# Projections and v products take turns over four PSUM banks until the retention's first step

## The chip, the core and the metric

The kernel runs on one core of one Trainium2 chip. Times are device microseconds of a whole execution. The engines are named as in the profile: PE is TensorE (PEld its weight loads), DVE is VectorE, ACT is ScalarE, POOL is GpSimd, SP issues transfers.

## What is computed

A model of two layers over 512 tokens of width 1024, in float32. Each layer normalises its input, projects it, runs three kinds of attention side by side (a retention with 4 heads in chunks of 128, a sparse attention with 4 heads that keeps the best 128 keys by an indexer's score, and a dilated attention with 8 heads), mixes them through an output matrix, and ends with an MLP.

```python
def hybrid_layer(x, attn_norm_w, w_in, ret_norm_w, kv_norm_w, w_uk, w_uv, w_out, mlp_norm_w, w_up, w_down, pos):
    h = rms_norm(x, attn_norm_w)
    proj = h @ w_in
    ret_cols, dsa_cols, dil_cols = jnp.split(proj, _offsets((RET_COLS, DSA_COLS, DIL_COLS)), axis=-1)
    mixed = jnp.concatenate([retention_mixer(ret_cols, ret_norm_w, pos),
                             dsa_mixer(dsa_cols, kv_norm_w, w_uk, w_uv),
                             dilated_mixer(dil_cols)], axis=-1)
    x = x + mixed @ w_out
    h = rms_norm(x, mlp_norm_w)
    return x + jnp.square(jax.nn.relu(h @ w_up)) @ w_down
```

## The kernel before

Every float32 operand is held as two parts, a rounded one (hi) and its remainder (lo), and each product is three matmuls (hi by hi, hi by lo, lo by hi). A projection (`proj`, L791) is one PSUM tile of 128 columns of weights by 512 tokens: 8 blocks of the inner dimension, 24 matmuls of 512 columns (`wform`, L329). A v product of the dilated heads (`dil_v`, L537) is one tile of 128 tokens by 256 columns: 24 matmuls of 256 columns (`tform`, L339); a call makes four of them, for four blocks of tokens.

PSUM's eight banks are three pools, made at L139 to L141: `mm` with two banks, `at` with four (scores, transposes, products of the heads), `rt` with two. The retention (`ret_tile`, L648) takes all its tiles from `rt`, and so do two of the four v products of each `dil_v`. All projections take `mm`. A bank is free for the next tile when its last reader is done. For a query (`evac_q`, L413) these are two steps of ACT (L423) and two of DVE (L424); for a key (`evac_k`, L428) two of ACT (L436) and two of DVE (L438), with two transfers that ACT issues; for a gate (`gate`, L634) a tanh on ACT (L644) and a step of DVE (L645), then one of POOL (L646); for a v product (`evac_v`, L514) a copy into a work buffer and a rounding, both on ACT (L520, L524), after which POOL takes the remainder from the work buffer (L526). There are three work buffers (pool `p`, `PB` = 3 at L50), which the heads' outputs and the gates use too.

The work of the attention is written head by head (loop in `attention`). Ahead of it stand the token parts, the indexer, the first selection round of the sparse attention (`topk`, L597, DVE only: L602 and L603) and `dil_v` for the first four heads, then query 0 and key 0. After the scores of head h the loop writes the steps that the list `FILL` (L53) names for it: query 1 after head 0; query 2, key 1 and key 2 after head 1; gate 0 after head 2; the second `dil_v` and gate 1 after head 3; key 3 after head 4; query 3 and the retention's own projection after head 5. Then come the products of the head before, as many steps of the retention as `RET` (L54) gives (none before h = 5, four there), and rounds of the selection.

The order on the engines is not that of the text: a planner builds each engine's queue ahead of time from priorities (position in the text plus the offsets of `PR`, L72) and its own estimate of when inputs and buffers are there. Each engine then runs its queue in order, and waits where an input or a buffer isn't ready.

Of the kernel before, what the change touches and what calls it, by code (L numbers as in the profile page):

```python
# [51 lines left out]
C = {  # L52
    'FILL': 'q1,q2 k1 k2,g0,d g1,k3,q3 r,v s0,w,s1,',  # L53
    'RET': (0, 0, 0, 0, 0, 4, 0, 3, 0, 1, 3, 1, 0),  # L54
    'TOPK': (1, 1, 0, 4, 0, 10, 0),
    'POOL_LO': ('dv', 'o', 'sq', 'rg', 'rqk', 'dq', 'dk', 'ukv'),
    'LSPLIT': 2,
    'HOLD': 6,
    'KS': ((4, 6), (0, 2)),
    'SK': 1,  # L60
# [63 lines left out]
class Kern:  # L124
# [412 lines left out]
    def dil_v(self, L, act, g):  # L537
        us = [(self.unit((L, "dv", g, k)), (k, k + 1, k + 2, k + 3)) for k in (0, 4)]
        for t in range(NT):
            ps = self.mm() if t < 2 else self.rt_bank()  # L540
            self.tform(us, act, t, ps, 256)
            self.evac_dil(ps[:, 0:256], g, t)
        self.done(2)
# [238 lines left out]
    def latent_k(self, L, pr):  # L782
# [5 lines left out]
            self.done()  # L788
        return self.evac_k(ps)

    def proj(self, key, act, cols=P):  # L791
        ps = self.mm()
        self.wform(self.unit(key), act, cols, ps, cols)
        self.done()
        return ps
# [34 lines left out]
    def attention(self, L, act):  # L830
        nc = self.nc
        A = self.A
        sc = None
        self.rt = [self.t(self.pmix, [P, 2, 1024], F32, "mix") for _ in range(2)]
        self.vd, self.sg, self.ct, self.vs, self.rqk_done = {}, None, None, None, False
        self.masks = self.t(self.psc, [P, N_CST - N_C1], F32, "masks")
        nc.sync.dma_start(self.masks, A["cst"][:, N_C1:])
# [54 lines left out]
        def out_part(h, t, ks, last=False):  # L892
            ps = self.mm()
            self.tform([(self.unit((L, "o", h, k)), (k, k + 1)) for k in ks], mix, t, ps)
            self.add_x(t, h, ps)
# [4 lines left out]
        for h in range(12 + C["SK"]):  # L900
            if h < 12:
                if h == 8:
                    self.bias(sc)
                with self.prio("hs", h):
                    self.head_s(heads[h // 2], h % 2)
            for f in fill.pop(0) if fill else ():
                with self.prio("fill", f):
                    steps[f]()
            if h == 8 + C["SK"]:
                for t in range(NT):  # L910
                    self.load_x(t, self.xd if L else A["x"])
                mix = [m0, None] + self.md
            if h >= 8 + C["SK"]:
                for _ in range(C["WO"]):
                    if wo and wo[0] not in hold:
                        assert 0 not in C["KS"][0] or m0_done
                        with self.prio("wo", h):
                            out_part(*wo.pop(0), C["KS"][0])
                            if wo and wo[0] == (1, 0):
                                self.done(len(C["KS"][0]))  # L920
            if h >= C["SK"]:
                with self.prio("hv", h):
                    self.head_v(heads[(h - C["SK"]) // 2], (h - C["SK"]) % 2)
            for _ in range(C["RET"][h] if h < 13 else 0):
                with self.prio("ret", h):
                    next(rets, None)
            if h < 6:
                with self.prio("topk", h):
                    self.topk(sc, C["TOPK"][h + 1])
# [200 lines left out]
```

## Time and profile before

| | us |
|---|---|
| median of 3 executions | 1236.36 |
| lowest, highest | 1236.02, 1240.37 |
| the profiled execution | 1236.08 |
| its span, first to last instruction | 1234.1 |
| PE busy (98% of the span) | 1207.2 |
| DVE busy (75%) | 921.4 |
| ACT busy (55%) | 679.2 |
| POOL busy (38%) | 472.4 |

The profile is of one execution. An engine's busy time is the time in which it has an instruction under way; a wait is the idle time just before an instruction, put down to the one that released it. The two layers repeat each other: in layer 0 the part from query 0 to the MLP's first matmul lies between 75 and 309.7 us, in layer 1 between 681 and 917.

### The profile page before, as it was taken

The page shows a single profiled execution, that of the slowest core. Times are in us where ns is not written, and L with a number is a line of the kernel's source. Part 1 is how long each engine was busy: PE and PEld are TensorE (multiplying, and loading weights), DVE is VectorE, ACT ScalarE, POOL GpSimd, SP SyncE. Part 2 cuts the span into 40 slices and gives each one's busy share as a digit, 9 for nine tenths or more (in the row PEclk, how much of TensorE's full clock was granted, in tenths as well). Part 3 has the DMA queues.
Part 4 walks back from the last instruction along what each step waited for, and adds up shares of the span by engine and source line. Part 5 has one row for each costly group of instructions (what it writes and reads, how often), then busy time and mean ns, then how long its engine had stood idle before and what let it go on. Part 6 is the DMA issues. An engine that isn't in the chain of part 4 may idle for free.

```text
span 1234.1 us, 16904 instructions
## 1 busy us (share of the span) xinstructions
PE 1207.2 (98%) x6116; PEld 1027.6 (83%) x6116; DVE 921.4 (75%) x1582; ACT 679.2 (55%) x1241; POOL 472.4 (38%) x461
## 2 busy tenths in 40 slices
PE   7999999999999999999999999999999999999997
PEld 5988888889888888888889888888898888888886
DVE  5599957776875966858866997687769668587596
ACT  6645758745644535535566456686465354354454
POOL 3453748553412304214224546664534032140232
PEclk9999999999999999999999999999999999999999
DMA  7432324215244061260153323231180622514201
GB/s 217 120 83 72 95 69 121 86 53 188 85 137 137 1 215 58 69 184 16 35 166 102 95 71 96 91 120 53 52 256 1 205 68 69 176 30 140 82 1 69
DMA packets 142180, 122.73 MB, mean 99 GB/s; under 512 B 6801, under 2 KB 114065, under 8 KB 142098
## 3 DMA queue, kind: packets, MB, share of 16 engines
q1 hardware_dynamic: 140178, 118.52, 31.9%
q10 hardware_dynamic: 1920, 3.15, 1.0%
q8 instruction: 48, 0.79, 0.3%
q14 instruction: 34, 0.28, 0.1%
HBM read 114.31 MB, written 4.19 MB: 96 GB/s over the span
## 4 chain that ended last, share of the span: by engine, by line
PE 85%; DVE 12%; ACT 1%; issue 1%; DMA 1%; SPq 0%; POOL 0%; POOLq 0%; DVEq 0%; ACTq 0%
PE mm L336 35%; PE mm L348 15%; PE rt L1036 14%; PE at L1036 7%; PE mm L1036 3%; DVE sc L603 3%; DVE top L602 3%; PE at L352 2%; PE at L491 2%; PE at L444 1%; PE at L443 1%; DVE ph L462 1%; PE at L336 1%; DVE Q L424 1%; DMA raw<-in_w_in_dram 1%
## 5 line engine op out<-in xcount | busy, mean ns | idle before, releaser
L336 PE MATMUL mm<-act,w 128*128 128x512 f32 (+2 forms) x2352 | 516.1, 377 | 3.1 <-DVE Q L424 3.1
L336 PEld LDWEIGHTS mm<-act,w 128*128 128x128 f32 x2352 | 424.4, 188 | 79.8 <-issue 3.9
L286 POOL TENSOR_TENSOR w<-raw,w 128x512 fp32r<-128x512 f32 (+1 forms) x124 | 160.0, 1313 | 99.2 <-ACT w L278 74.0
L278 ACT CAST w<-raw 128x1024 fp32r<-128x1024 f32 (+1 forms) x138 | 142.9, 1037 | 79.2 <-PE rt L1036 27.6
L1036 PE MATMUL rt<-w,U 128*128 128x512 f32 x768 | 183.2, 389 | 0.0
L286 DVE TENSOR_TENSOR w<-rd,w 128x1024 fp32r<-128x1024 f32 x112 | 144.7, 1304 | 50.0 <-ACT w L278 50.0
L286 DVE TENSOR_TENSOR w<-raw,w 128x1024 fp32r<-128x1024 f32 (+1 forms) x76 | 94.0, 1238 | 107.5 <-ACT w L278 107.2
L1036 PEld LDWEIGHTS rt<-w,U 128*128 128x128 f32 x768 | 144.1, 188 | 29.9
L993 POOL TENSOR_TENSOR st<-s 128x256 f32<-128x256 f32 x32 | 39.1, 1223 | 330.1 <-ACT s L982 325.3
L278 ACT CAST w<-rd 128x1024 fp32r<-128x1024 f32 x112 | 117.6, 1050 | 83.4 <-PE rt L1036 41.7
L348 PE MATMUL mm<-w,act 128*128 128x456 f32 (+2 forms) x576 | 118.4, 351 | 3.0 <-DVE act L400 1.8
L348 PEld LDWEIGHTS mm<-w,act 128*128 128x128 f32 x576 | 96.4, 189 | 15.2 <-DVE act L400 2.8
L348 PE MATMUL mm<-w,mix 128*128 128x512 f32 x384 | 97.3, 401 | 0.6 <-DVE Q L424 0.5
L1036 PE MATMUL at<-w,U 128*128 128x512 f32 (+1 forms) x396 | 97.7, 386 | 0.0
L304 DVE TENSOR_TENSOR rd<-rd,rd 128x1024 f32<-128x1024 f32 x64 | 94.3, 1473 | 0.5
L1036 PEld LDWEIGHTS at<-w,U 128*128 128x128 f32 x396 | 73.6, 188 | 15.0
L980 ACT ACTIVATE s<-mm 128x512 f32<-128x512 f32 x62 | 36.9, 595 | 84.2 <-PE mm L336 74.5
L348 PEld LDWEIGHTS mm<-w,mix 128*128 128x128 f32 x384 | 70.5, 190 | 15.2 <-DVE Q L424 0.9
L997 ACT CAST U<-st 128x1024 fp32r<-128x1024 f32 x32 | 33.7, 1054 | 80.9 <-POOL st L994 80.9
L991 POOL TENSOR_TENSOR st<-s,s 128x256 f32<-128x256 f32 x32 | 36.7, 1146 | 92.0 <-ACT s L982 92.0
L463 ACT ACTIVATE ph<-ph,sm 128x128 f32<-128x128 f32 (+1 forms) x96 | 53.9, 562 | 24.5 <-DVE sm L462 23.8
L998 DVE TENSOR_TENSOR U<-s,U 128x256 fp32r<-128x256 f32 x64 | 63.9, 998 | 0.0
(169 smaller groups left out, 1766.4 us busy)
## 6 DMA issues: line engine op xcount, KB each, us to landing
raw<-in_w_up_dram SPq DMA_DIRECT2D x64, 512.0 KB, 4.2
rd<-in_w_down_dram SPq DMA_DIRECT2D x32, 1024.0 KB, 5.1
raw<-in_w_in_dram SPq DMA_DIRECT2D x48, 512.0 KB, 3.9
raw<-in_w_out_dram SPq DMA_DIRECT2D x16, 512.0 KB, 3.9
xv<-in_x_dram SPq DMA_DIRECT2D x7, 512.0 KB, 4.8
KH<-KH ACTq DMA_DIRECT2D x24, 128.0 KB, 2.3
raw<-in_w_in_dram SPq DMA_DIRECT2D x8, 256.0 KB, 2.9
xd<-xv SPq DMA_DIRECT2D x4, 512.0 KB, 3.9
```

The lines of the kernel that those rows point to most:

```text
L278: self.nc.scalar.copy(hi, src)
L286: eng.tensor_tensor(lo[:, i:i + step], src[:, i:i + step], hi[:, i:i + step].bitcast(F32), op=ALU.subtract)
L304: sub = lambda o, a, b: self.nc.vector.tensor_tensor(o, a, b, op=ALU.subtract)
L336: self.nc.tensor.matmul(ps[:cols, toks[0]:toks[1]], a, b, start=(k == 0 and j == 0), stop=(k == KB - 1 and j == 2))
L348: self.nc.tensor.matmul(ps[:, :w], a, b, start=(n == 0), stop=(n == tot - 1))
L463: nc.scalar.activation(p, p, AF.Exp, bias=a, scale=-1.0, accum_out=b)
L602: nc.vector.max(m, sc[b])
L603: nc.vector.match_replace(sc[b], m, sc[b], SENT)
L980: nc.scalar.activation(s, ps, AF.Relu)
L993: tt(st[:, 2], a[:, 0], a[:, 1], op=ALU.subtract)
L998: nc.vector.tensor_tensor(lo, src, hi.bitcast(F32), op=ALU.subtract)
L1036: nc.tensor.matmul(ps[:, c0:c1], a, w, start=(new and n == 0), stop=(n == 11), skip_group_check=True)
```

## The change

A counter, set to zero at the start of each layer's attention, counts the tiles of `proj` and `dil_v`. The third and the fourth of every four take a bank of `rt`, the others one of `mm`. From the first retention step on (a flag set where the loop comes to h = 5, behind that head's fill steps) all take `mm`. The other users of the pools (the retention, the token parts, the retention's own projection, the latent keys and values, the output matrix, the MLP) are left as they are.

```diff
--- before.py
+++ after.py
@@ -537,7 +537,7 @@
     def dil_v(self, L, act, g):
         us = [(self.unit((L, "dv", g, k)), (k, k + 1, k + 2, k + 3)) for k in (0, 4)]
         for t in range(NT):
-            ps = self.mm() if t < 2 else self.rt_bank()
+            ps = self.bank()
             self.tform(us, act, t, ps, 256)
             self.evac_dil(ps[:, 0:256], g, t)
         self.done(2)
@@ -788,8 +788,13 @@
             self.done()
         return self.evac_k(ps)
 
+    def bank(self):
+
+        self.nbank += 1
+        return self.rt_bank() if self.nbank % 4 in (3, 0) and not self.ret_started else self.mm()
+
     def proj(self, key, act, cols=P):
-        ps = self.mm()
+        ps = self.bank()
         self.wform(self.unit(key), act, cols, ps, cols)
         self.done()
         return ps
@@ -832,6 +837,7 @@
         A = self.A
         sc = None
         self.rt = [self.t(self.pmix, [P, 2, 1024], F32, "mix") for _ in range(2)]
+        self.nbank, self.ret_started = 0, False
         self.vd, self.sg, self.ct, self.vs, self.rqk_done = {}, None, None, None, False
         self.masks = self.t(self.psc, [P, N_CST - N_C1], F32, "masks")
         nc.sync.dma_start(self.masks, A["cst"][:, N_C1:])
@@ -921,6 +927,7 @@
             if h >= C["SK"]:
                 with self.prio("hv", h):
                     self.head_v(heads[(h - C["SK"]) // 2], (h - C["SK"]) % 2)
+            self.ret_started = self.ret_started or C["RET"][h] > 0
             for _ in range(C["RET"][h] if h < 13 else 0):
                 with self.prio("ret", h):
                     next(rets, None)
```

## Rows read from the trace of the kernel before

**Rows 1.** The page: busy time, share of the span, instructions; a group of matmuls.

```profile
PE 1207.2 (98%) x6116; PEld 1027.6 (83%) x6116; DVE 921.4 (75%) x1582; ACT 679.2 (55%) x1241; POOL 472.4 (38%) x461
...
L1036 PE MATMUL rt<-w,U 128*128 128x512 f32 x768 | 183.2, 389 | 0.0
```

**Rows 2.** Waits of PE: who waited for whom, us in total, times, longest.

```profile
PE mm L336 <- DVE Q L424: 3.1, 2, 1.6
...
PE rt L352 <- DVE rw L733: 1.5, 2, 0.7
PE rt L673 <- ACT rT L664: 1.3, 2, 0.7
PE mm L348 <- DVE KL L438: 1.2, 2, 0.6
PE rt L673 <- DVE rT L665: 1.1, 2, 0.5
PE at L491 <- ACT PT L485: 1.0, 4, 0.3
PE rt L690 <- POOL rP L679: 0.6, 3, 0.3
PE mm L778 <- DVE P L623: 0.6, 2, 0.3
PE mm L348 <- DVE Q L424: 0.5, 2, 0.2
```

**Rows 3.** Stretches: length, busy PE, PEld, DVE, ACT, POOL, clock, DMA.

```profile
75.00:147.00 72.00, 69.56 (x377) 59.59 (x376) 71.10 (x216) 41.12 (x88) 38.38 (x39) 1.00 0.32 89
147.00:188.00 41.00, 41.00 (x212) 34.92 (x211) 20.87 (x62) 23.15 (x53) 21.94 (x27) 1.00 0.26 72
188.00:309.70 121.70, 118.39 (x726) 102.71 (x725) 91.48 (x218) 77.58 (x175) 66.79 (x73) 1.00 0.38 117
309.74:611.00 301.26, 301.26 (x1330) 249.44 (x1330) 225.98 (x212) 148.47 (x193) 80.10 (x66) 1.00 0.30 91
...
262.00:272.00 10.00, 8.53 (x54) 7.06 (x53) 7.52 (x14) 4.86 (x12) 5.89 (x7) 1.00 0.35 100
868.00:879.00 11.00, 9.79 (x54) 8.16 (x53) 7.71 (x15) 4.71 (x11) 5.91 (x7) 0.84 0.32 91
```

**Rows 4.** PE in order of time, layer 0: start, us, instructions, idle before.

```profile
75.25 11.07 PE L336 MATMUL mm<-act,w 128*128 128x512 f32 x48
87.89 5.70 PE L336 MATMUL mm<-act,w 128*128 128x512 f32 x24 [1.57 <-DVE Q L424]
...
101.00 1.59 PE L348 MATMUL rt<-w,act 128*128 128x256 f32 x12
...
129.93 3.10 PE L348 MATMUL mm<-w,act 128*128 128x256 f32 x24 [0.61 <-DVE KL L438]
```

**Rows 5.** DVE in order of time: steps that free a bank.

```profile
87.05 0.69 DVE L424 SCALAR_TENSOR_TENSOR Q<-mm,Q 64x512 fp32r<-64x512 f32 x1
...
100.28 0.69 DVE L424 SCALAR_TENSOR_TENSOR Q<-mm,Q 64x512 fp32r<-64x512 f32 x1
...
129.09 0.69 DVE L438 TENSOR_TENSOR KL<-mm,KH 64x512 fp32r<-64x512 f32 x1
...
132.37 0.67 DVE L645 SCALAR_TENSOR_TENSOR P<-P,mm 128x512 f32<-128x512 f32 x1
```

**Rows 6.** The stretch before the retention, tile rt alone: length, PE, PEld, DVE, ACT.

```profile
75.00:188.00 113.00, 7.28 (x52) 6.66 (x50) 0.00 (x0) 2.49 (x8) 1.00 0.30 83
```

**Rows 7.** ACT in order of time: the v products' copies to a work buffer.

```profile
134.16 0.38 ACT L520 COPY P<-mm 128x256 f32<-128x256 f32 x1
...
137.45 0.35 ACT L520 COPY P<-mm 128x256 f32<-128x256 f32 x1
...
139.91 0.37 ACT L520 COPY P<-rt 128x256 f32<-128x256 f32 x1 [0.39 <-POOL xv L526]
...
144.74 0.37 ACT L520 COPY P<-rt 128x256 f32<-128x256 f32 x1
```

## The prediction

> **What bounds the kernel now.** I read the page's busy times first. TensorE is busy for 1207.2 of 1234.1 us [rows 1], so 26.9 us of the span is without a matmul, part of it at the start and the end. The change removes no matmul and adds none, so it can only move this idle time. The waits of TensorE come second [rows 2]: of the middle of the kernel they name 3.1 us in two waits on the vector step of a query's split (L424), 1.2 us in two waits on the vector step of a key's split (L438), and seven smaller entries (1.5, 1.3, 1.1, 1.0, 0.6, 0.6 and 0.5 us, 6.6 us together) that stand in the retention and around the heads. The two layers do the same work, so each wait of one layer has its twin in the other. Third come the stretches [rows 3]: from 75 to 147 us TensorE is idle for 72.00 - 69.56 = 2.44 us while VectorE is busy for 71.10 of 72.00; from 147 to 188 TensorE never stops; from 188 to 309.7 it stops for 3.31 us; in the MLP not at all. So in the stretch that the change touches two engines are nearly full, and TensorE's stops come from VectorE being late with its half of an eviction.
>
> The order on TensorE shows where [rows 4]. Query 0 and key 0 are one run of 48 matmuls from 75.25 to 86.32. Then TensorE waits 1.57 us, because query 1 needs one of the two mm banks, and query 0's is free only when its second L424 ends at 87.05 + 0.69 = 87.74 [rows 5]. The second wait, 0.61 us, stands before the run of 24 at 129.93, the first v product of the second half on an mm bank; key 2's bank comes free at 129.09 + 0.69 = 129.78 [rows 5]. Meanwhile the retention's banks are nearly unused: between 75 and 188 us TensorE spends 7.28 us on them [rows 6].
>
> **The change, part by part.** No instruction is added; the counter is Python. The counter runs 1 to 4 over the first four v products (mm, mm, rt, rt, as before), 5 and 6 over query 0 and key 0 (mm), 7 and 8 over queries 1 and 2 (rt), 9 and 10 over keys 1 and 2 (mm), 11 over gate 0 (rt), 12 to 15 over the second four v products (rt, mm, mm, rt instead of mm, mm, rt, rt), 16 over gate 1 (rt), then keys and queries of pair 3 (mm). From the first retention step on all is as before. Per layer five tiles move from mm to rt and one from rt to mm.
>
> The trace agrees with each pool serving its requests in program order, from whichever buffer is free: the v products on rt run at 101.00 [rows 4], those on mm, whose place in the program is ahead of them, only at 129.93, behind two keys and a gate. I work with that.
>
> *Removed: query 1's wait for query 0.* It asks for an rt bank, which the first four v products left before 86.3 (the last of their matmuls is ahead of the run at 75.25). 1.57 us per layer, 3.1 us in both [rows 2].
>
> *Removed: the v product's wait for key 2.* Its first one now asks for rt. 0.61 us per layer, 1.2 us in both [rows 2].
>
> *Added: five waits of the same kind, each two tiles further back.* A projection is 24 matmuls; from the run of 48, (11.07 - 0.39)/47 = 0.227 us each, 5.45 us a tile (0.39 us is how long one matmul of 512 columns stands in the page [rows 1]). A v product on rt is half as wide; by the run of 24 at 129.93 it takes about 2.8 us without its pipeline's tail. The lag from the last matmul of a tile to its bank being free is, for query 1, from 87.89 + 5.70 = 93.59 [rows 4] to 100.28 + 0.69 = 100.97 [rows 5]: 7.4 us. With TensorE going straight on at 86.3, queries 1 and 2 and keys 1 and 2 end at 91.8, 97.2, 102.7 and 108.1. Gate 0 wants query 1's bank at 108.1 and it is free at 99.2; the first v product wants query 2's at 113.6 (free 104.6), the second key 1's at 116.4 (free 110.1), the third key 2's at 119.2 (free 115.5), the fourth gate 0's at 122.0 (free 113.6 + 7.4 = 121.0). The head work that lies in between pushes the wants back and not the lags. So all five cost nothing at the lag of before, with 1.0 to 9.0 us in hand; what hides them is the two tiles that now lie between. Bounds: 0, and, if VectorE answers twice as late (14.8 us), 128.4 - 122.0 = 6.4 us a layer at the last of them. I take 0, as six evictions were all over by 129.8 before too [rows 5].
>
> *Added: v products on both mm banks.* Their eviction is ScalarE and GpSimd through one work buffer, in order: ScalarE's copies come at 134.16, 137.45, 139.91 and 144.74 [rows 7], the first after the gate's buffer is free (its VectorE step is at 132.37) [rows 5]. Key 3 waits behind the second copy on an mm bank. If that chain starts no earlier than before, TensorE, 2.18 us ahead, has done all else at about 135 and key 3 could go at about 138: up to 3.2 us. Gate 1 covers it: it needs only the first product's rt bank, and is 5.45 us long. I take 0, bound 3.2 us a layer.
>
> *Moved: weights and transfers.* A weight buffer comes free when its projection ends, so ScalarE's and GpSimd's split of later weights and the load behind it on SP's queue start up to 2.2 us earlier. ScalarE and GpSimd are 41.12 and 38.38 us busy in 72 [rows 3], the DMA share is 0.32: no cost, and nothing of the path gains, as no wait of TensorE in the middle names a weight or a load [rows 2].
>
> *Retention.* Its first step asks for a bank after gate 1, and TensorE's use of rt starts again only at 188; 0.
>
> *The order behind it.* A planner lays each queue out anew, so the 6.6 us of smaller waits can shrink or grow; bounds -6.6 and, as a doubling, +6.6. I take 0. Nearby the clock falls once: 0.84 granted from 868 to 879, 1.00 in the twin stretch of layer 0 with the same waits [rows 3]. Between the levels of 2.4 and 1.2 GHz, 0.84 means 32% of 11 us at the lower, 3.5 us that did the work of 1.8. So 1.8 us can be won in one layer, or lost in the other; I take 0.
>
> Sum: 1236.08 - 3.1 - 1.2 = 1231.8 for the profiled execution. It lies 0.28 us under the median of 1236.36, so 1232 for the median.
>
> What the busy time of TensorE is worth has to be asked, since all this calls it full. From 75 to 147 weight loads fill 59.59 us, 82.8% of 72; in the MLP, where no wait exists, 249.44 of 301.26, also 82.8% [rows 3]. The Trainium skill ("Perfetto Trace Analysis", Identifying the Most-Contended Engine) says that matmul busy time is a poor measure of how near TensorE is to its limit, and to take the weight loads' share: by it 17% would be left here. The rows don't bear that out as room that banks could open, because the share is the same where banks never hold TensorE.
>
> **The rivals.**
> - *Given back to VectorE.* It is busy for 71.10 of 72 us [rows 3]; what TensorE gains at 86.3 it loses at the next thing that only VectorE can hand over, a head's scores or a key. For: both waits end on VectorE. Against: 129.93 was such a gate and cost 0.61 us only, and v products need no VectorE. Result 1236.
> - *The smaller waits go too.* TensorE reaches the later gates 2.2 us ahead, VectorE has caught up by then (20.87 of 41 us busy from 147 to 188) [rows 3], and the chains find their inputs ready. Half of 6.6 + 1.8 us on top: 1236.4 - 4.3 - 4.2 = 1228; all of it 1223.7. Against: those waits are inside the retention's own chain of steps, which an earlier start moves along.
> - *Slower: evictions queue up on VectorE.* Four tiles instead of two are ready for the same full VectorE at 92 to 108 us, its queue is in order, and the selection rounds stand between; the lag doubles to 14.8 us. Place: the fourth v product behind gate 0. Price 6.4 us a layer: 1236.4 - 4.3 + 12.8 = 1245. It decides from a lag of 7.4 + 1.0 = 8.4 us on; break-even with before at 10.6 us. For: the fullness of VectorE. Against: the sum of its work is unchanged, and evictions start earlier.
> - *Room inside TensorE's busy time.* If 17% of 72 us could be opened in both layers, 2 x 12.4 us, the time would be 1212. That is what the skill's measure above would make of it; the equal 82.8% speak against.
> - *It doesn't do what it says:* the queues are laid out so that query 1 doesn't run ahead, though its bank is free. 1236.
>
> **How the numbers follow.** Forecast 0.42 (1229 to 1235 around 1232), given back 0.22, smaller waits too 0.16, slower by lag 0.15, room inside 0.01, no effect 0.04. The measurement tells 0.5% or 6.2 us from no change: under 1230.2 is faster, over 1242.5 slower. Faster: 0.05 of the forecast's, 0.14 of the third's and the 0.01: 0.20. Slower: 0.12 of the lag's and 0.03 of the given-back's, when chains behind grow: 0.15. The rest, 0.65, is within 0.5%. The range goes from 1227 (half of the smaller waits and the clock won) to 1243 (a lag of 13.8 us); about 0.07 lies below and 0.12 above.
>
> **What would show it.** Right: query 1's run follows key 0's with no gap at 86.3, in both layers; the waits on L424 and L438 before an mm or rt tile are under 0.5 us a layer; the tile rt shows queries and gates between 86 and 130; TensorE's idle time from 75 to 147 falls from 2.44 us to under 0.5; layer 1's 681 to 753 alike. Given back: the same gap, later, on a scores matmul (L443) behind VectorE. Wrong by lag: waits on L424, L438 or L645 before an rt tile, over 2 us each, at 115 to 130. Wrong in the order behind: the stretch from 188 to the MLP holds more than its 3.31 us.

## The result: slower by 1.15%, and most of it where the diff touches nothing

After the change the kernel takes 1251.09 us (median of 4, 1249.68 to 1252.79), beside 1237.26 us for the kernel before on the same chip: a ratio of 1.0115, 95% interval 1.0094 to 1.0135. The profiled execution took 1249.68 us, its span is 1247.9 us.

TensorE's line of the page, against [rows 1]: 7.1 us busier with the same 6116 matmuls, and the rest of the 13.8 us more idle.

```profile
PE 1214.3 (97%) x6116; PEld 1030.3 (83%) x6116; DVE 919.2 (74%) x1582; ACT 679.6 (54%) x1241; POOL 473.3 (38%) x461
```

TensorE's waits in the whole kernel, against [rows 2]. The columns are as there.

```profile
PE at L491 <- ACT PT L485: 4.2, 6, 1.1
PE rt L348 <- DVE P L645: 2.9, 2, 1.5
...
PE rt L673 <- ACT rT L664: 1.4, 2, 0.7
PE rt L352 <- DVE rw L733: 1.3, 2, 0.7
PE mm L348 <- DVE Q L424: 1.1, 2, 0.5
...
PE at L443 <- DVE PT L486: 0.7, 2, 0.4
PE rt L336 <- DVE Q L424: 0.6, 1, 0.6
```

The two waits that the sum took off are gone: 3.1 us on L424 before an mm projection, and 1.2 us on L438 before a v product. In their place stand 2.9 us on L645 before a v product on a retention bank, and a head's products (L491) wait 4.2 us for L485 instead of 1.0. (Lines behind the new method stand some lines later in the changed kernel: its L833 is L828 of before.)

For all that follows I cut each layer at three places that are easy to find in time: TensorE's first matmul of query 0, its first transpose of the retention (L352, rt from mix), and the MLP's first matmul. The last is at 291.04 us in layer 0 of the kernel before: the 309.7 that I gave ahead of the prediction is where the MLP's matmuls of 512 columns begin, and TensorE runs through from the one to the other. Between the first two lie 585 matmuls, between the last two 569, the same in every kernel here. Rows of stretches, columns as in [rows 3] (length first, then TensorE's busy time, granted clock third from the end), of the kernel before, layer 0 and layer 1:

```profile
75.25:188.18 112.93, 110.49 (x587) 94.44 (x586) 91.90 (x277) 64.20 (x138) 60.25 (x65) 1.00 0.30 83
188.18:291.04 102.86, 99.58 (x571) 84.19 (x570) 81.33 (x201) 68.06 (x157) 61.08 (x69) 1.00 0.27 83
681.52:794.48 112.96, 110.57 (x588) 94.46 (x587) 91.91 (x277) 64.21 (x138) 60.27 (x65) 1.00 0.30 83
794.48:898.35 103.87, 100.85 (x572) 85.39 (x570) 81.13 (x201) 67.86 (x157) 61.07 (x69) 0.98 0.27 82
```

and of the kernel after:

```profile
75.61:189.11 113.50, 110.85 (x588) 94.41 (x586) 91.92 (x277) 64.17 (x138) 60.51 (x65) 1.00 0.29 82
189.11:296.85 107.74, 102.59 (x572) 85.65 (x570) 78.91 (x201) 68.37 (x157) 61.45 (x69) 0.98 0.27 79
687.37:803.57 116.20, 112.62 (x587) 95.97 (x586) 93.71 (x277) 64.06 (x138) 60.26 (x65) 0.99 0.29 81
803.57:912.41 108.84, 103.16 (x572) 85.60 (x570) 78.41 (x201) 67.88 (x157) 61.87 (x69) 0.98 0.27 79
```

Of the loss, 4.9 and 5.0 us lie between the retention and the MLP, where every bank is as before; 0.6 and 3.2 us lie in the stretch that the diff touches. The rest is unchanged: from the MLP's first matmul in layer 0 to query 0 of layer 1 it is 681.52 - 291.04 = 390.5 us before and 687.37 - 296.85 = 390.5 us after.

TensorE in order of time, layer 0 of the kernel after, against [rows 4]:

```profile
75.61 11.07 PE L336 MATMUL mm<-act,w 128*128 128x512 f32 x48
86.52 8.10 PE L336 MATMUL rt<-act,w 128*128 128x512 f32 x35
...
112.20 3.69 PE L336 MATMUL rt<-act,w 128*128 128x512 f32 x15
...
127.25 2.11 PE L336 MATMUL rt<-act,w 128*128 128x512 f32 x8
```

```profile
130.19 0.51 PE L491 MATMUL at<-PT,xv 128*128 128x512 f32 x1 [0.84 <-ACT PT L485]
...
134.41 3.14 PE L348 MATMUL rt<-w,act 128*128 128x256 f32 x24 [1.45 <-DVE P L645]
```

The run at 86.52 follows key 0's without a gap, as predicted, though most of it is query 2's. The fourth v product waits at 134.41 for gate 0's bank, the place that the slower rival named. TensorE's idle time from 75 to 147 us, which was to fall from 2.44 us to under 0.5, is 72.00 - 69.35 = 2.65. Gate 0's 24 matmuls are torn apart: 15 at 112.20, one at 116.55, and the last 8 at 127.25, behind three v products.

```profile
75.00:147.00 72.00, 69.35 (x378) 59.46 (x377) 71.26 (x217) 42.13 (x88) 39.20 (x41) 1.00 0.32 89
```

### The profile page after: what moved, and what is told of

The parts are those of the page before. It is cut to its first block, busy times and chain, and to the rows that moved or that the text cites. A ratio compares the mean times of both kernels' runs of the same rounds, so it can differ in the third digit from the quotient of the medians.

```text
span 1247.9 us, 16872 instructions
## 1 busy us (share of the span) xinstructions
PE 1214.3 (97%) x6116; PEld 1030.3 (83%) x6116; DVE 919.2 (74%) x1582; ACT 679.6 (54%) x1241; POOL 473.3 (38%) x461
## 4 chain that ended last, share of the span: by engine, by line
PE 85%; DVE 10%; ACT 2%; issue 1%; POOL 1%; DMA 0%; SPq 0%; POOLq 0%; DVEq 0%; ACTq 0%
PE mm L336 35%; PE rt L1043 14%; PE mm L348 13%; PE at L1043 7%; PE mm L1043 3%; PE at L352 2%; DVE sc L603 2%; DVE top L602 2%; PE rt L336 2%; PE at L491 2%; PE at L444 2%; PE at L443 1%; PE rt L348 1%; PE at L336 1%; DVE PT L486 1%
## 5 line engine op out<-in xcount | busy, mean ns | idle before, releaser
L336 PE MATMUL mm<-act,w 128*128 128x512 f32 (+2 forms) x2160 | 472.1, 376 | 0.0
L336 PEld LDWEIGHTS mm<-act,w 128*128 128x128 f32 x2160 | 389.2, 188 | 69.3
L286 DVE TENSOR_TENSOR w<-raw,w 128x1024 fp32r<-128x1024 f32 (+1 forms) x76 | 95.0, 1251 | 106.2 <-ACT w L278 106.0
L348 PE MATMUL mm<-w,act 128*128 128x456 f32 (+2 forms) x576 | 117.8, 351 | 2.2 <-DVE act L400 2.2
L348 PEld LDWEIGHTS mm<-w,act 128*128 128x128 f32 x576 | 96.5, 189 | 14.4 <-DVE act L400 3.2
L348 PE MATMUL mm<-w,mix 128*128 128x512 f32 x384 | 98.6, 403 | 2.1 <-DVE Q L424 1.1
L348 PEld LDWEIGHTS mm<-w,mix 128*128 128x128 f32 x384 | 70.6, 191 | 17.2 <-PE rt L352 1.5
```

What stands on the lines that cost most here:

```text
L286: eng.tensor_tensor(lo[:, i:i + step], src[:, i:i + step], hi[:, i:i + step].bitcast(F32), op=ALU.subtract)
L336: self.nc.tensor.matmul(ps[:cols, toks[0]:toks[1]], a, b, start=(k == 0 and j == 0), stop=(k == KB - 1 and j == 2))
L348: self.nc.tensor.matmul(ps[:, :w], a, b, start=(n == 0), stop=(n == tot - 1))
```

## The experiments

Theory 1: the loss is in the order in which the planner now lays the queues, and the banks only set that off. Theory 2: the banks themselves, held longer and turned differently. Where an order is "held", edges of order (no wait on a semaphore) tie each listed instruction to the one before it on its engine. The planner still lays what isn't listed, so where TensorE alone is held the queues of the other engines are laid anew around it:

```diff
+def hold(tc, chains):
+    ins = {i.name: i for i in tc.nc.cur_bb.bb.instructions}
+    info = mybir.DependencyInfo(mybir.DependencyClass.NoSync, mybir.DependencyReason.DATA)
...
+        for p, n in zip(names, names[1:]):
+            tc.add_manual_dep(ins[n], p, info, reason="hold")
...
         hybrid_kernel(tc, A, out)
+        hold(tc, CHAINS)
```

The stretches of all runs, in us; in brackets what VectorE's third mask step (L593, beside query 0) took in that layer, of which more below. An asterisk marks a stretch whose granted clock is under 1.00.

| run | query 0 to retention, layers 0 and 1 | retention to MLP, layers 0 and 1 | ratio to before, 95% interval |
|---|---|---|---|
| before | 112.9 (1.42), 113.0 (1.43) | 102.9, 103.9* | 1 |
| after | 113.5 (0.28), 116.2* (1.42) | 107.7*, 108.8* | 1.0115 (1.0094 to 1.0135) |
| 1 | 114.6 (1.43), 113.6 (0.28) | 105.7*, 103.8 | 1.0041 (1.0025 to 1.0058) |
| 2 | 111.8 (0.28), 111.8 (0.28) | 107.4*, 109.2* | 1.0068 (1.0046 to 1.0090) |
| 3 | 114.4* (1.42), 111.7 (0.27) | 102.8, 107.8* | 1.0035 (1.0016 to 1.0054) |
| 4 | 114.3 (1.42), 113.2 (0.28) | 103.8*, 103.9* | 1.0013 (1.0000 to 1.0027) |
| 5 | 113.1 (1.43), 113.1 (1.43) | 108.9*, 107.7* | 1.0085 (1.0060 to 1.0110) |
| 6 | 112.8 (0.28), 112.8 (1.43) | 102.9, 104.0* | 1.0013 (1.0000 to 1.0025) |
| 7 | 115.7 (1.43), 117.3* (1.43) | 107.5*, 110.7* | 1.0130 (1.0110 to 1.0149) |
| 8 | 113.0 (1.43), 113.0 (1.43) | 110.7*, 110.6* | 1.0077 (1.0050 to 1.0105) |
| 9 | 113.0 (1.42), 111.9 (0.27) | 102.8, 103.8* | 1.0002 (0.9983 to 1.0021) |
| 10 | 111.7 (0.28), 112.8 (1.43) | 102.8, 107.0* | 0.9999 (0.9984 to 1.0014) |
| 11 | 116.1* (1.43), 114.4* (0.28) | 106.8, 107.7* | 1.0110 (1.0085 to 1.0134) |
| 12 | 113.5 (0.28), 116.1* (1.42) | 110.3*, 107.0* | 1.0105 (1.0076 to 1.0135) |
| 13 | 114.7 (1.42), 116.3* (1.43) | 106.9*, 107.6* | 1.0093 (1.0078 to 1.0109) |
| 14 | 113.6 (0.27), 116.1* (1.42) | 107.8*, 107.9* | 1.0087 (1.0062 to 1.0112) |
| 15 | 111.8 (0.27), 112.9 (1.42) | 107.0*, 103.8* | 1.0000 (0.9984 to 1.0017) |
| 16 | 111.8 (0.28), 111.8 (0.28) | 102.8, 103.9* | 0.9971 (0.9957 to 0.9985) |

The clock falls more often in some executions than in others, and each profile is of one. So I also take (1 - granted clock) x length off each late stretch. That leaves 101.8 to 103.8 us wherever TensorE has the order of before, and 104.4 to 107.1 us wherever it has another. Two stretches that look long in the order of before, run 10's layer 1 and run 15's layer 0, are long by a granted clock of 0.95 alone: 107.0 us become 101.9 and 101.8.

### Order or banks: runs 1, 2 and 5

Run 1, the edit: CHAINS lists TensorE's instructions of the kernel before from the retention to the MLP, laid on the changed kernel.

> The changed kernel with one thing added: from the retention's first transpose to the MLP's first matmul, in both layers, TensorE is made to run its 569 matmuls in the order in which the kernel before ran them (edges of order only; every bank is where the change put it, and the stretch ahead of the retention keeps the change's order). What was lost there is 4.9 and 5.0 us (102.9 and 103.9 before, 107.7 and 108.8 after). Theory 1, the loss is in the order: both stretches come back to 103 to 104 us, the fall of the granted clock in them goes, and the whole is 1251 - 10 = 1241 us. Theory 2, the loss is in the banks (the retention's banks come to it late, or in another turn): order or not, 107 to 109 us each and 1249 to 1253 us.

Measured: 1243.45 us. Layer 1 is back at 103.8 us. Layer 0 stands at 105.7, but at a granted clock of 0.97; (1 - 0.97) x 105.7 is 3.2 us, so the order gives its part back there too. The fall of the clock, which was to go with it, didn't go.

Run 2, the edit: the same list for the changed kernel's order, laid on the kernel before.

> The mirror of it: the kernel before, its banks untouched, with TensorE made to run the same stretch of both layers in the order of the changed kernel (100 and 108 of 569 matmuls stand elsewhere). Theory 1, the order: 107 to 109 us in both stretches, 1237 + 10 = 1247 us, with the last head's products standing bare behind the used-up output matrices. Theory 2, the banks: 103 to 104 us in both and 1237 us.

Measured: 1245.69 us, with both stretches long and no bank changed:

```profile
75.26:187.04 111.78, 110.50 (x588) 94.45 (x586) 90.75 (x277) 64.20 (x138) 60.39 (x65) 1.00 0.30 84
187.04:294.43 107.39, 102.25 (x571) 85.43 (x570) 78.84 (x201) 68.05 (x157) 61.40 (x69) 0.98 0.26 79
684.82:796.61 111.79, 110.51 (x587) 94.43 (x586) 90.75 (x277) 64.19 (x138) 60.40 (x65) 1.00 0.30 84
796.61:905.78 109.17, 104.05 (x572) 86.90 (x570) 79.18 (x201) 67.82 (x157) 61.88 (x69) 0.97 0.26 79
```

Run 5 leaves the banks and the planner alone and only turns one of its weights:

```diff
-    'PR': {... 'fill_g1': -100, ...},
+    'PR': {... 'fill_g1': 100, ...},
```

> The kernel before with no bank changed at all: one weight in the planner's table, that of gate 1's place ('fill_g1'), goes from -100 to 100, and the planner lays everything anew. 68 of 585 matmuls ahead of the retention stand elsewhere, and from the retention to the MLP the order falls within 3 and 11 matmuls (of 569) of the changed kernel's. Theory 1, the loss is the planner's other order, whatever sets it off: 107 to 109 us in both stretches, and with 112 to 114 us ahead of them 1245 to 1248 us. Theory 2, it takes the new banks: 103 to 104 us in both, 1236 to 1239 us.

Measured: 1248.41 us, 10 us slower than the 1238.35 us of before on the same chip, and the second and fourth row show where:

```profile
77.51:190.63 113.12, 110.71 (x587) 94.33 (x586) 93.70 (x278) 65.24 (x139) 59.42 (x65) 1.00 0.29 82
190.63:299.50 108.87, 103.92 (x570) 86.83 (x570) 78.60 (x201) 67.89 (x156) 62.01 (x69) 0.97 0.27 79
690.02:803.14 113.12, 110.71 (x587) 94.33 (x585) 93.69 (x278) 65.24 (x139) 59.45 (x65) 1.00 0.29 82
803.14:910.82 107.68, 102.74 (x570) 85.65 (x570) 78.35 (x201) 67.84 (x156) 62.05 (x69) 0.98 0.27 80
```

Theory 1 holds for the later stretch, and theory 2 falls there: the loss comes and goes with the order, on either set of banks. Nothing about banks is needed to set it off. It is the kernel before that is special: the disturbances ahead of the retention in runs 5, 7, 8 and 11, and in one layer of run 3, all end in one other order, about 100 of 569 matmuls away and the same within a dozen, and that order is 5 us a layer longer (less the clock, 3.2 and 4.9 us in the changed kernel). Why the planner's table of weights suits the one order of before so well isn't shown.

### The change in parts: runs 3, 7, 8 and 11

Run 3 against the kernel before; the planner is free in all four runs:

```diff
 def proj(self, key, act, cols=P):
-    ps = self.mm()
+    ps = self.rt_bank() if key[1:3] in (("dq", 1),) else self.mm()
```

> The kernel before with one projection moved to the retention's banks, query 1; every other projection and all v products stay where they were. The planner is left free: in layer 0 it lays the stretch from the retention to the MLP as before, in layer 1 as in the changed kernel but for 8 matmuls of 569. Theory 1, the order: 103 us in layer 0 and 108 to 109 us in layer 1, from the same banks. Theory 2, the banks: both alike, 103 to 104 us if query 1 does no harm. Ahead of the retention, my sum said -1.57 us a layer (111.4 us instead of 112.9), the rival that gives it back to VectorE 112.9. Whole by theory 1: 1237 - 3 + 5 = 1239 us.

Measured: 1241.27 us. One kernel, one set of banks, and the late stretch is 102.8 us in layer 0 (old order) and 107.8 in layer 1 (other order), as theory 1 said. Query 1's wait is gone in both layers, but a v product on the retention's bank then waits for query 1, 0.3 us in layer 1 and here in layer 0:

```profile
111.27 4.61 PE L348 MATMUL rt<-w,act 128*128 128x256 f32 x24 [2.40 <-DVE Q L424]
```

Run 7 puts the four projections on the retention's banks (the tuple above with dq 1, dq 2, rg 0 and rg 1), the v products stay.

> Half of the change: the four projections that it moves (queries 1 and 2, gates 0 and 1) on the retention's banks, the v products on the banks of the kernel before. Planner free; from the retention to the MLP its order is the changed kernel's but for 3 and 5 matmuls. Theory 1: 107 to 109 us there in both layers. Ahead of it, if the wait of the fourth v product for gate 0's bank (1.45 us) is the price of the v products' new banks, it is gone and the stretch takes 111.5 to 112.5 us; if the projections on the retention's banks make it, the third or fourth v product, still on those banks, waits 1.4 us or more and the stretch takes 113.5 us or more. Whole 1246 to 1252 us.

Measured: 1254.62 us, above the range expected and no different from the whole change within the intervals. The fourth v product waits 1.5 us for gate 0 in both layers though its bank is the old one: the second branch of the expectation. Run 8 moves only the v products' second half, against the kernel before:

```diff
-            ps = self.mm() if t < 2 else self.rt_bank()
+            ps = self.rt_bank() if t in (0, 3) and g else self.mm() if g or t < 2 else self.rt_bank()
```

> The other half: all projections on the banks of before, and the four later v products in the change's turn (retention's, projections', projections', retention's instead of projections' twice and then the retention's twice). Planner free. Theory 1: the other order from the retention to the MLP and 107 to 109 us in both layers. Ahead of it, with no projection on the retention's banks, no v product waits behind gate 0: 111.5 to 113 us, by whether the mask step of line 593 takes 0.28 or 1.42 us. Whole 1244 to 1247 us. By theory 2, 103 to 104 us from the retention on and 1237 us.

Measured: 1246.35 us. Ahead of the retention nothing is lost or won (113.0 us at 1.43), the waits on L424 and L438 stand as before (1.6 and 0.6 us), and the other order costs its part behind (110.7 and 110.6 us, at a granted clock of 0.95 and in the longest of four executions, 1253.62 us). So the loss ahead of the retention comes with the projections, and the v products' new banks cost nothing there. The planner laid the order ahead of the retention anew in both runs, so that bank and order aren't told apart in this stretch.

Run 11, against the changed kernel:

```diff
-    def bank(self):
+    def bank(self, rt=True):
...
-        ps = self.bank()
+        ps = self.bank(key[1] != "rg")
```

> The changed kernel, with the two gates back on the projections' banks (queries 1 and 2 and the v products stay where the change put them). If gate 0's hold on a retention bank is the price ahead of the retention, the wait of the last v product (1.45 us behind line 645) is gone and that stretch takes 112.0 us with the mask step of line 593 at 0.28 us and 113.2 us with 1.42 us (after: 113.5 and, without its clock fall, 114.5). If the v products then wait as long for query 1 or 2, 113.5 us or more. From the retention on the planner's other order again: 107 to 109 us in both layers. Whole 1246 to 1249 us.

Measured: 1250.04 us. The wait behind L645 falls to 0.5 us in layer 0, but the scores of a head wait 2.0 and 1.5 us for VectorE's L462 instead. Less the clock, at about 1.8 us a fall (below), the stretch is 114.3 us with the step at 1.43 and 112.7 us with 0.28: between the two branches. That fits a gate 0 that carries part of the price and a VectorE that takes part of it back; with the planner free it isn't shown.

### Is a wait worth its length: runs 4, 6, 9 and 10

Run 4 is run 3 with TensorE held to the order of before from query 0 to the MLP, run 6 the same from the retention on.

> Query 1 alone on the retention's banks, and TensorE made to run both layers from query 0 to the MLP in the order of the kernel before, so that only the wait for the bank is gone. By the step of my sum: each layer shorter by the 1.57 us of that wait, 111.4 us from query 0 to the retention, 1237 - 3.1 = 1234 us. By the rival that VectorE takes it back at the next bank: 112.9 us in both layers, 1237 us.

> Query 1 alone on the retention's banks, the planner free up to the retention and TensorE held to the order of the kernel before from there to the MLP. By theory 1: 103 to 104 us in both stretches, so some 5 us under the run with query 1 alone (1241.3), 1236 us. Ahead of the retention the third causal mask step on VectorE (line 593, beside query 0) comes out at 1.42 or at 0.28 us: with 1.42 us 112.8 us from query 0 to the retention, with 0.28 us 111.7 us. If query 1's bank gains anything beyond that, 111 us or less.

Measured: 1239.58 and 1240.12 us. Both late stretches are back at 103 to 104 us. Ahead of them run 4 is 1.4 us a layer longer than before at the same L593 step, not 1.57 shorter, and above both branches of its expectation: the first v product that shares query 1's bank waits, and longer than query 1 did. VectorE's queue is that of before up to this wait; behind it the planner moved some of its steps too, and the later v product's wait for key 2 grew from 0.6 to 1.3 us, so not all of the 1.4 us is the bank's.

```profile
101.26 0.36 PE L348 MATMUL rt<-w,act 128*128 128x256 f32 x1 [2.84 <-DVE Q L424]
```

Run 6 missed its expectation in layer 0: L593 took 0.28 us there and the stretch still took 112.8 us, not 111.7. With query 1's bank nothing is gained beyond L593's two values in either run.

Runs 9 and 10 take the same waits away with no bank at all, by moving VectorE's eviction steps ahead in its queue (both engines' orders held in all else):

```diff
 # VectorE, layer 0 (layer 1 alike)
+L424 SCALAR_TENSOR_TENSOR Q<-mm,Q      (query 0, first half)
 L602 MAX top<-sc   x3
-L424 ...                               (first half)
+L424 SCALAR_TENSOR_TENSOR Q<-mm,Q      (query 0, second half)
 L603 MATCH_REPLACE sc<-top,sc   x3
 L602 MAX top<-sc
-L424 ...                               (second half)
```

> The kernel before, no bank changed: on VectorE the two eviction steps of query 0 (line 424, which free the bank that query 1 waits for) are moved ahead of three and four maxima of the top-k selection, in both layers, and TensorE and VectorE are held to the order of before in all else. It takes away the same wait (1.57 us, or 0.42 us where the mask step of line 593 takes 0.28 us) without another bank and without another order. By the step of my sum that a wait is worth its length: 111.4 us from query 0 to the retention in both layers, whichever way the mask step falls, the late stretches as before (103 to 104 us), and 1235 to 1236 us as a whole. By the rival that VectorE takes it back at the next bank: no wait there, but 112 to 113 us all the same and 1238 us.

> As the run before it, and the second eviction step of key 2 (line 438), behind which a v product waits 0.61 us, moved ahead of two replacement steps of the selection. By the step of my sum: 110.8 us from query 0 to the retention, another 1.2 us off the whole, 1234 to 1235 us. By the rival: no further gain, 1236 us or more.

Measured: 1236.73 and 1237.61 us, no change in either against 1236.90 on the same chip. The whole times alone would hardly decide it, the stretches do. In run 9 queries 0 and 1 and key 0 are one run of 72 matmuls, and then the next projection waits for key 0's bank, 1.50 us in layer 0; the v product later waits 1.24 instead of 0.61:

```profile
94.79 4.78 PE L336 MATMUL mm<-act,w 128*128 128x512 f32 x20 [1.50 <-DVE KL L438]
```

```profile
130.20 3.11 PE L348 MATMUL mm<-w,act 128*128 128x256 f32 x24 [1.24 <-DVE KL L438]
```

The stretch keeps its length to 0.15 us, 113.0 and 111.9 in run 9, 111.7 and 112.8 in run 10, though run 10 has the v product's wait down to 0.3 us too. My step falls, and the rival "given back to VectorE" holds: the wait was VectorE's lateness showing at the first place where TensorE needed it.

### What that lateness is: runs 15 and 16

In the table one number orders the early stretch on the banks of before: 112.8 to 113.1 us where L593's third step took 1.42 us, 111.7 to 111.9 where it took 0.28. On the banks of the whole change it is 113.5 to 113.6 and, where the clock didn't fall, 114.6 to 114.7 us. Of the first 32 layers traced (16 kernels) 20 have the long form and 12 the short, none lies between. In the kernel before GpSimd starts a pair of remainders beside it; VectorE's row first, then GpSimd's:

```profile
75.45 1.42 DVE L593 SCALAR_TENSOR_TENSOR sc<-masks,sc 128x128 f32<-128x128 f32 x1
```

```profile
75.43 2.59 POOL L286 TENSOR_TENSOR w<-raw,w 128x512 fp32r<-128x512 f32 x2
```

Run 15 adds a wait to the kernel before, with every engine held to its order; run 16 puts it on both instructions of the pair:

```diff
+    sync = mybir.DependencyInfo(mybir.DependencyClass.Sync, mybir.DependencyReason.DATA)
+    for p, n in ((MASK3_L0, REM_A_L0), (MASK3_L1, REM_A_L1)):      # run 15
+    for p, n in ((MASK3_L0, REM_A_L0), (MASK3_L0, REM_B_L0), (MASK3_L1, REM_A_L1), (MASK3_L1, REM_B_L1)):   # run 16
+        tc.add_manual_dep(ins[n], p, sync, reason="hold")
```

> The kernel before, every engine held to its order, with one wait added in each layer: GpSimd starts the pair of weight remainders (line 286) that falls beside the third mask step of VectorE (line 593) only when that step is done, so that the step doesn't run beside them. If VectorE's lateness paces the stretch from query 0 to the retention: the step takes 0.28 us in both layers, query 1 waits 0.4 us instead of 1.57, the stretch takes 111.8 us instead of 112.9 in both layers, and the median falls by what the step costs on the average so far (1.42 us in 20 of 32 layers traced, 0.28 us in the others: 2 x 1.14 x 0.6 = 1.4 us), 1236.5 us against 1238. If the wait is only moved by it: 112.9 us and no change of the whole.

> As the run before it, with the wait for the third mask step (line 593) on both instructions of the GpSimd pair (line 286), so that neither can run beside it. If VectorE's lateness paces the stretch from query 0 to the retention: 0.28 us for the step and 111.8 us for the stretch in both layers, and 1236.5 us as a whole (2 x 1.14 x 0.6 = 1.4 us under the kernel before). If not: 112.9 us in at least one layer with the step at 0.28 us, and 1238 us.

Run 15 missed: the wait came to stand on the second of the pair, the first still ran beside the step in layer 1 (1.42 us, 112.9 us), and the time is that of before. Run 16 does it: 1234.08 us against 1237.91, the fastest kernel here and faster than both. The step, GpSimd's pair behind it (the profile puts the end of its wait down to ScalarE's L524; the step itself ends at 75.31, 0.13 us ahead of the pair), and the stretches:

```profile
75.03 0.28 DVE L593 SCALAR_TENSOR_TENSOR sc<-masks,sc 128x128 f32<-128x128 f32 x1
```

```profile
75.44 2.56 POOL L286 TENSOR_TENSOR w<-raw,w 128x512 fp32r<-128x512 f32 x2 [0.39 <-ACT xv L524]
```

```profile
74.83:186.61 111.78, 110.49 (x588) 94.47 (x586) 90.72 (x277) 64.22 (x138) 60.31 (x65) 1.00 0.30 84
...
680.09:791.89 111.80, 110.53 (x588) 94.48 (x587) 90.72 (x277) 64.22 (x138) 60.29 (x65) 1.00 0.30 84
```

Both layers are at 111.8 us and query 1's wait is 0.42 us instead of 1.57. So a VectorE step for which no matmul waits directly moves the layer by its own 1.14 us, and the removal of a TensorE wait of 1.57 us by nothing. The stretches explain 2.3 us against the profiled execution of before (2 x 1.15) and 1.4 us on the average. The median fell by 3.8, and most of that goes with the clock: it was 0.9973 on the mean of the 12 executions of run 16 and 0.9949 on that of the 17 of before beside them, and 0.0024 x 1236 is 3.0 us. Whether the clock fell less often because of the shorter step isn't shown.

### Where in the other order: runs 12, 13 and 14

TensorE's 25 us around the last heads, in the kernel before and in run 2 (other order, same banks):

```profile
250.00:275.00 25.00, 23.53 (x138) 19.99 (x137) 19.43 (x39) 10.70 (x22) 12.31 (x13) 1.00 0.20 64
```

```profile
250.00:275.00 25.00, 21.86 (x114) 17.64 (x112) 14.51 (x31) 10.03 (x21) 12.30 (x14) 0.93 0.23 64
```

24 matmuls fewer, while VectorE falls from 19.43 to 14.51 us busy. The changed kernel shows it in order of time:

```profile
261.57 0.69 PE L491 MATMUL at<-PT,vs 128*128 128x384 f32 x4
...
263.22 0.38 PE L491 MATMUL at<-PT,vs 128*128 128x256 f32 x1 [0.82 <-ACT PT L485]
263.84 2.34 PE L348 MATMUL mm<-w,mix 128*128 128x512 f32 x9 [0.24 <-DVE xv L833]
...
268.60 1.30 PE L491 MATMUL at<-PT,vs 128*128 128x384 f32 x5 [0.45 <-DVE PT L486]
...
273.24 2.63 PE L348 MATMUL mm<-w,mix 128*128 128x512 f32 x6
```

The output matrices (L348 from mix) are what TensorE has to do while a head's softmax runs. In the other order 33 of them, with the retention's state products in between, come right ahead of the last products, which then stand bare. The last row is one more price: six matmuls took 2.63 us there, 1.66 us in the kernel before; the granted clock had fallen behind the idle time.

Run 12 lays 30 of these matmuls back between the products (31 of 569 change places), run 13 moves the 34 matmuls of the retention's third chunk to their earlier places, run 14 does both; all on the changed kernel, its order held in all else.

> The changed kernel with its own order held from the retention to the MLP in both layers, but for one place: between the last retention state steps and the mixing of the last chunk, 31 of 569 matmuls change places, so that the state products go first and 30 output-matrix matmuls (line 348 from mix) are laid between the last two heads' products, 12, 9 and 9, as the kernel before has them; in the changed kernel 21 of these run in one go ahead of the products. The rest of its other order stays. If the loss is the missing cover at this place (114 matmuls in 25 us against 138 in the run that has the other order on the banks of before): 103.5 to 104.5 us in both layers instead of 107.7 and 108.8, and 1251 - 8 = 1243 us. If the loss lies in the whole other order (some 100 matmuls that stand elsewhere before this place): 106 us or more, and 1248 us or more.

> The changed kernel with its own order held from the retention to the MLP in both layers, but for the 34 matmuls of the retention's third chunk (places 253 to 429 of 569): they stand where the kernel before has them, 11 places and more earlier, and the other matmuls there keep their order among themselves. If the retention's chain sets the end (its transposes, scores and state products, and the steps on VectorE, ScalarE and GpSimd behind them, start late in the other order): 103.5 to 105 us in both layers and 1251 - 8 = 1243 us. If it is the heads' products that stand bare: 107 us or more, their waits at line 491 as in the changed kernel (1.1 and 0.5 us), and 1249 us or more.

> The two edits together: the retention's third chunk at its earlier places and the output-matrix matmuls back between the last two heads' products (12, 9 and 9). If both are needed: 103 to 104 us in both layers, 1242 to 1243 us, and the run with the retention's chunk alone lies above it. If the retention's chunk alone is the cause, no faster than that run. If it takes the whole order: 106 us or more and 1248 us.

Measured: 1250.94, 1248.95 and 1249.10 us. None brings the time back. In run 12 the products wait 1.4 us in one piece instead of 1.6 in three, and the retention's L673 then waits 1.9 us for ScalarE's L664 instead of 0.7: ScalarE and VectorE have been laid anew as well, and the stop moves one step on. In run 14 the wait of the products falls to 0.4 us, L673's is 1.4 us, and the granted clock of both stretches is 0.97. Less the clock run 14's stretches are 104.4 and 104.5 us, beside 106.0 and 107.1 after and 102.9 and 102.2 before: the two edits together win about half of the loss, and the clock of this execution takes it again. So the cause is the order (runs 1, 2 and 5), the loss shows at the last heads, but which part of the order makes it stays open; neither part that I moved gives all of it back.

## Why the prediction was wrong

*"Query 1's wait, 1.57 us per layer", and the v product's 0.61.* Both waits went, as the trace of after shows, and taking them away without a bank was worth nothing (runs 9 and 10). I had VectorE at 71.10 of 72 us busy [rows 3] and read TensorE's idle 2.44 us as what a bank could win. On a stretch where the other engine is full, a bank moves the wait to the next place where that engine is needed. This was the first rival, at 0.22, though its time, 1236, missed as well. The size was luck besides: 1.14 of the 1.57 us came from one step that took 1.42 us in both layers of the execution shown, and takes 0.28 in 12 layers of 32.

*"All five cost nothing."* The fourth v product waits 1.45 us behind gate 0, in both layers: the slower rival's place, but not its mechanism. That rival wanted a lag above 8.4 us. Gate 0's last matmul ends at 127.25 + 2.11 = 129.36, its bank is free when VectorE's step ends at 133.70 + 0.66 = 134.36, 5.0 us later. In the kernel before gate 0 had the same lag, from 125.58 + 2.33 = 127.91 (first row, TensorE before) to 132.37 + 0.67 = 133.04 [rows 5], 5.1 us; my 7.4 was a query's. The second row is VectorE's step after:

```profile
125.58 2.33 PE L336 MATMUL mm<-act,w 128*128 128x512 f32 x9
```

```profile
133.70 0.66 DVE L645 SCALAR_TENSOR_TENSOR P<-P,rt 128x512 f32<-128x512 f32 x1
```

What failed is the table of ends: I let the tiles run one after another, 91.8, 97.2, 102.7, 108.1, and the planner didn't. Query 2 runs ahead of query 1, query 1 ends at 102, and gate 0's last third comes behind three v products, right ahead of the fourth. Ahead of the retention the whole change costs 1.7 us a layer at the same L593 step (113.5 against 111.8, 114.6 against 112.9). Run 4 shows that a bank can cost such a thing with TensorE's order held. The old order ahead of the retention on all the new banks was not tried, so how the 1.7 us divide between bank and order stays open.

*"The order behind it: bounds -6.6 and +6.6. I take 0."* This is the term that made the sign: +4.9 and +5.0 us. Taking 0 supposed that the order behind would stay as good as it was, and nothing in the trace of before said so. The bound doubled the waits that this trace names, and counted idle time alone. Idle time grew by 4.5 us (5.15 + 5.68 against 3.28 + 3.02), inside the bound, most of it at a place without a wait before, the last heads' products. The other 5.4 us are TensorE busy longer with the same matmuls: 1.8 of them are one more fall of the clock, and for the rest I have no cause. What I wrote as a sign of it, more than 3.31 us idle from 188 to the MLP, is what after shows: 107.74 - 102.59 = 5.15 us.

*The clock, "I take 0".* The profile of before has one fall in the middle [rows 3], that of after three, each behind a cluster of waits (much the same waits as those before the second fall, at 130 to 134 us in layer 0, had none behind them):

```profile
266.00:282.00 16.00, 13.92 (x72) 11.18 (x71) 12.05 (x26) 6.71 (x16) 6.61 (x9) 0.89 0.14 43
740.00:760.00 20.00, 17.06 (x89) 14.42 (x87) 19.94 (x60) 13.26 (x30) 13.15 (x14) 0.91 0.23 67
876.00:892.00 16.00, 12.86 (x67) 10.11 (x66) 12.62 (x27) 8.41 (x19) 8.38 (x9) 0.89 0.33 99
```

(1 - 0.89) x 16 and (1 - 0.91) x 20 are 1.8 us each, the size that I had bounded one with.

Together, for the profiled executions: 2 x 1.7 us ahead of the retention, less 1.1 for L593's short form in layer 0 of after, 4.9 + 5.0 less the 1.8 of one more fall for the order behind, and 2 x 1.8 for two falls more: 3.4 - 1.1 + 8.1 + 3.6 = 14.0 of 1249.68 - 1236.08 = 13.6 us.

*"The smaller waits go too"* was wrong in sign, and *"room inside TensorE's busy time"* finds nothing: weight loads fill 59.46 us of the 72 from 75 to 147 after, 59.59 before [rows 3].

## What to carry to other kernels

Where two engines are full together, price a wait by the other engine's lateness, not by its length: ask where that engine is needed next, and try a version that removes the wait without the change. In a kernel whose order a planner lays out, any edit redraws every queue behind it, so hold the old order once on the new kernel and the new order once on the old: two runs split the edit from the redrawing. Before a duration of one execution goes into a sum, look for the same step in the twin layers of other traces.

## What was not expected of the hardware

One VectorE step of 128x128 elements takes 0.28 or 1.42 us where a GpSimd instruction begins at the same moment. Which it becomes can't be read from the starts: 75.45 beside 75.43 us in the long form above, 75.47 beside 75.44 in run 2, where it took 0.28. With GpSimd idle, the first of the three mask steps takes 0.29 us in every layer traced. The Trainium skill ("SBUF — State Buffer", SBUF: two separate sides) says that a VectorE step with two inputs from SBUF and a GpSimd step that reads SBUF share a pair of ports, and that the one that starts first keeps it for its whole instruction. The trace agrees: this step has two such inputs, the remainders read SBUF, and the 1.14 us more are near the 1.30 of one remainder (2.59 for two). It agrees the other way round too: where the step is short it is GpSimd that takes longer, 2.70 us for the pair in run 2 instead of 2.59. VectorE's row of run 2 first, then GpSimd's:

```profile
75.47 0.28 DVE L593 SCALAR_TENSOR_TENSOR sc<-masks,sc 128x128 f32<-128x128 f32 x1
```

```profile
75.44 2.70 POOL L286 TENSOR_TENSOR w<-raw,w 128x512 fp32r<-128x512 f32 x2
```

And the second mask step, which always starts 0.34 us behind a GpSimd step (L526), takes 0.83 us in every layer traced. That the long form can be avoided by a wait on GpSimd's pair (run 16) is measured.

The granted clock of the late stretch is under 1.00 in 11 of 18 profiles in layer 0 and in 17 of 18 in layer 1, in the order of before as in the other. TensorE's idle time doesn't tell which: it fell in run 1's layer 0 with 2.98 us idle and stayed at 1.00 in run 11's with 5.56. At 1.7 us and more a fall, two profiles are compared less the clock or not at all.
